# A hybrid recurrent and attention block on one core: the head's fillers, norm gain and first weights, and one copy at the entry of the up-projection

## The chip, the core and the metric

The kernel runs on one core of one Trainium2 chip. The metric is the device time of one execution in microseconds (us); of several runs the median is taken. Before the change it is 912.32 us (three runs, 912.11 to 912.33).

The engines are named as in the profile: PE is TensorE's matmul, PEld its weight load, DVE VectorE, ACT ScalarE, POOL GpSimd, SP SyncE. A "q" behind a name is the engine's sequencer, which waits and issues DMAs.

## What is computed

One layer over 512 tokens of 1024 channels, in float32:

```
h = rms_norm(x, mix_norm_pre)                 # x * rsqrt(mean(x^2) + eps) * gain
xa, ga, q, k, v, f, gA, gB = split(h @ w_in)
y_a = gelu(ga) * rg_lru(causal_conv4(xa));  y_b = forgetting_attention(q, k, v, f)
m = sigmoid(gA) * (y_a @ P_A) + sigmoid(gB) * (y_b @ P_B)
x = x + rms_norm(m @ w_out, mix_norm_post)
h = rms_norm(x, ffn_norm_pre)
up = causal_conv3(h @ w_up);  gate, val = split(up)
x = x + rms_norm((gelu(gate) * val) @ w_down, ffn_norm_post)
```

## The kernel before

**Arithmetic.** Every float32 product is made of three products in the reduced-precision type float32r. An operand `a` is split into a high part `ah` (a copy that rounds, `hi`, usually on ACT) and a low part `al = a - ah` (`lo`, on DVE or POOL), and `a*b` becomes `ah*bh + ah*bl + al*bh`. The class `Split` (L154) holds a block of weights: `raw` from DRAM by a DMA on SP (L166), `wh` from `hi` (L172), `wl` from `lo` (L175).

**Order of the work.** The stages stand one behind the other: the head (norm of x, its turning, and the first four blocks `xa0` to `xa3` of the input projection), then the rest of that projection with the recurrent gates, the attention, the merge, the output projection, the up-projection with conv and GLU, and the down-projection. Most of it is put in order by a scheduler that models times. The head (L576 to L685) and the up-projection from its entry on (L1373 to the end) stand under `manual_schedule`: each engine runs its instructions in the order in which the code gives them. An instruction that waits holds up all that stand behind it on its engine.

**The head** (L576 to L685). Token tiles `xt0` to `xt3` (128 tokens x 1024) and the first weights come in by SP's DMAs, the gain row `gone` (1 x 1024) by one of ACT's. What stands around the change:

- `spin(n)` (L594): n fillers on PE, products of nothing that is used, written into the bank that `xa3` takes later. Before, each is `ident x ident` in float32, 128 columns. `spin(6)` stands ahead of the gain products, `spin(1)` behind them.
- The gain row has to stand on all 128 partitions. DVE splits each half of `gone` into `gh` and `gl` of one row (L604, L605). PE multiplies a row of ones with them (L607), K = 1, so that a bank `pgain[i]` holds the half-row 128 times.
- Per token tile, `sumsq_whole` (L611) squares and sums on ACT and takes `rstd_of` (L237 and L239); `scaled` (L619) makes `x * rstd * gain` on DVE in two halves; `turn` (L246) transposes each half in four 128x128 pieces on PE into a bank; `evac_hi` (ACT, L250) copies it to `hh`, `evac_lo` (DVE, L254) the remainder to `hl`.
- `by_kind(0, X, ...)` (L638) multiplies block `xa0` with tokens 0 to 255 (`X`), kind after kind: `hh*wh`, then `hl*wh`, then `hh*wl`, eight products of 256 columns each. Its weights `wh_xa0` are rounded by ACT (`us[0].hi()`), `wl_xa0` is made by POOL (`us[0].lo(pool)`). Then `half(1, X)` does `xa1` (L230, L231, L233), and tiles 2 and 3 are turned.

**The entry of the up-projection** (L1373 to L1404). The up-projection uses a seven-product scheme on halves (class `Pair`, L341). `p.p5()` makes product 5 into the left half of bank `p.c`; `p.keep(1, ...)` (L436) copies that half to SBUF on ACT. In the first `period` (L454) PE goes on with `p.product(6, ...)` into the other bank, ACT keeps that one too (`keep(0)`), and `p.product(3, p.c[:, X])` then adds onto the half that `keep(1)` must have copied. `m.plain_low(0)` and `m.plain_high(0)` prepare weights of a later pair `m`: an ACT copy with a sign (L364), a DMA on POOL that adds onto it (L365), and an ACT copy that rounds (L380). `first_tap(0)` is two ACT instructions (L1325) on the first blocks.

Of the kernel before, what the change touches and what calls it, by code (L numbers as in the profile page):

```python
# [8 lines left out]
F32 = mybir.dt.float32  # L9
F32R = mybir.dt.float32r  # L10
BF16 = mybir.dt.bfloat16
AF = mybir.ActivationFunctionType
ALU = mybir.AluOpType
# [3 lines left out]
P = 128  # L17
S = 512
D = 1024
KD = D // P  # L20
# [43 lines left out]
def kernel(  # L64
# [16 lines left out]
    act, dve, pool, pe = nc.scalar, nc.vector, nc.gpsimd, nc.tensor  # L81
# [17 lines left out]
    def bank(name):  # L99
        return pspools[-1].tile([P, 512], F32, tag="ps", name=name)  # L100
# [4 lines left out]
    HALVES = (slice(0, 512), slice(512, 1024))  # L105

    ident = cpool.tile([P, P], F32, name="ident")
# [144 lines left out]
    def turned_lo(pv, t, g, ah, al):  # L252
        dst = (slice(None), slice(4 * g, 4 * g + 4), slice(t * P, (t + 1) * P))
        return dve.tensor_tensor(out=al[dst], in0=pv, in1=ah[dst].bitcast(F32), op=ALU.subtract)  # L254
# [67 lines left out]
    KH, SH = KD // 2, S // 2  # L322
# [5 lines left out]
    X, Y = slice(0, SH), slice(SH, S)  # L328
# [170 lines left out]
    with ExitStack() as rg:  # L499
        rt, ixt, tt = {}, {}, {}  # L500
        last_act = [None]
        with ExitStack() as r0:
            xpool = r0.enter_context(tc.tile_pool(name="xc", bufs=6, reuse_waits="tile"))
            gwpool = r0.enter_context(tc.tile_pool(name="rgw", bufs=2, reuse_waits="tile"))
            xc, xh, xl = {}, {}, {}
# [65 lines left out]
            with tc.tile_pool(name="pre", bufs=2, side="right", reuse_waits="tile") as pre, ExitStack() as wp:  # L571
# [6 lines left out]
                gone = pre.tile([1, D], F32, name="gone", bufs=1)  # L578
# [5 lines left out]
                us = [Split(*order[t][1:], order[t][0], wpre) for t in range(2)]  # L584
# [7 lines left out]
                pw = pss[3]  # L592

                def spin(n):  # L594
                    for i in range(n):
                        pe.matmul(pw[:, P * (i % 4) : P * (i % 4) + P], ident, ident, start=True, stop=True)

                spin(6)
                pgain = [bank(f"gain{i}") for i in range(2)]
                one = xpool.tile([P, S], F32R, tag="xc", name="one")[0:1, :P]  # L600
                pool.memset(one.bitcast(F32), 1.0)
                for i, c in enumerate(HALVES):
                    gh, gl = (xpool.tile([P, S], F32R, tag=x, name=f"gain_{x}{i}")[0:1] for x in ("xh", "xl"))
                    dve.tensor_copy(out=gh, in_=gone[:, c])  # L604
                    dve.tensor_tensor(out=gl, in0=gone[:, c], in1=gh.bitcast(F32), op=ALU.subtract)  # L605
                    for j, g in enumerate((gh, gl)):
                        pe.matmul(pgain[i], one, g, start=j == 0, stop=j == 1)  # L607

                xns, rss, ptr, lasts = {}, {}, {}, [None, None]

                def sumsq_whole(t):  # L611
                    xns[t] = pre.tile([P, D], F32, tag="xn", name=f"xn{t}")
                    ss = small.tile([P, 1], F32, tag="ss", name=f"ss_p{t}")
                    act.activation(out=xns[t], in_=xts[t], func=AF.Square, accum_out=ss)
                    rss[t] = rstd_of(ss, f"p{t}")
# [9 lines left out]
                def evac_hi(t, g):  # L625
                    lasts[0] = turned_hi(ptr[t, g], t, g, hh)

                def evac_lo(t, g):
                    lasts[1] = turned_lo(ptr[t, g], t, g, hh, hl)
# [4 lines left out]
                def by_kind(i, c, kinds):  # L634
                    wh, wl = us[i].parts()
                    for n, (w, h, k0, k1) in enumerate(kinds):
                        for k in range(k0, k1):
                            pe.matmul(pss[i][:, c], (wh, wl)[w][:, k], (hh, hl)[h][:, k, c],  # L638
                                      start=n == 0 and k == k0, stop=n == len(kinds) - 1 and k == k1 - 1)

                spin(1)
                sumsq_whole(0)
                scaled(0, 0)
                scaled(0, 1)
                turn(0, 0)
                turn(0, 1)
                sumsq_whole(1)
                us[0].hi()
                us[0].lo(pool)
                evac_hi(0, 0)  # L650
                evac_hi(0, 1)
                for g in range(2):
                    scaled(1, g)
                    turn(1, g)
                for g in range(2):
                    evac_lo(0, g)
                for g in range(2):
                    evac_hi(1, g)
                    evac_lo(1, g)
                by_kind(0, X, ((0, 0, 0, KD), (0, 1, 0, KD), (1, 0, 0, KD)))  # L660
                us[1].hi()
                us[1].lo(pool)
                sumsq_whole(2)
# [258 lines left out]
    with ExitStack() as g2:  # L922
# [17 lines left out]
        p, n = gp[0], gp[1]  # L940
# [39 lines left out]
    with ExitStack() as at:  # L980
# [141 lines left out]
        i = KD - 2  # L1122
# [38 lines left out]
    xpool = fstk.enter_context(tc.tile_pool(name="x2", bufs=1, reuse_waits="tile"))  # L1161
# [18 lines left out]
    with ExitStack() as mix:  # L1180
# [116 lines left out]
        with ExitStack() as later:  # L1297
            for i in turned[NT - 1]:
                later.enter_context(tc.issue_after(i.ins))
            p = pairs[NU]  # L1300
# [61 lines left out]
    def first_tap(j):  # L1362
        fe[j] = [tap(e, first[2 * j + i][0], t) for i, (e, t) in enumerate(((j, "cg"), (j + JF, "cv")))]

    def first_taps(j, *which):
        for i in which or (0, 1):
            taps(j + JF * i, first[2 * j + i][0], fe[j][i])
# [7 lines left out]
    p, n = pairs[NU], pairs[NU + 1]  # L1375
# [18 lines left out]
    p.add(p.a[:, X], p.a[:, X], 2)  # L1394
    first_tap(0)
    n.sums_lo(1)
    m.plain_low(0)
    m.plain_high(0)
    p.p5()
    p.keep(1, p.c[:, X])  # L1400
    first_taps(2)
    first_taps(0, 0)
    m.sums(0)
# [64 lines left out]
    with man2:  # L1468
# [3 lines left out]
        b, p = pairs.pop(JF - 2), pairs.pop(JF - 1)  # L1472
# [274 lines left out]
```

## Time and profile before

| what | value |
|---|---|
| median of the runs | 912.32 us |
| the profiled execution's own time | 910.93 us |
| its span, first to last instruction | 909.2 us |
| PE, PEld busy | 899.7 us (99%), 801.4 us (88%) |
| DVE, ACT, POOL busy | 736.5 (81%), 596.3 (66%), 214.8 us (24%) |
| chain that ended last | PE 98%, ACT 1%, DMA 1% |
| DMA | 185.24 MB, 204 GB/s over the span |

Times in the views are from the start of the span. In a row of a timeline stand the start, the length, the engine, the line, the operation, what it writes and reads, the shapes and how many were merged; behind it in brackets the idle time before it and what ended it. In a row of waits stand who waited for whom, the total, how often, and the longest. A matmul's length in such rows holds its way through the array, so that consecutive ones overlap: their rate is read from their starts.

### The profile page before, as it was taken

How to read it: one execution, taken by the hardware profiler on the slowest of the kernel's cores; microseconds unless marked ns; L12 is line 12 of the kernel's file. 1: busy time of each engine (PE TensorE's matmuls, PEld its weight loads, DVE VectorE, ACT ScalarE, POOL GpSimd, SP SyncE). 2: the span in 40 equal slices, each digit the busy share in tenths (PEclk: the TensorE clock that was granted, in tenths of full speed). 3: DMA queues.
4: the chain of work that ended last, by engine and by line, in shares of the span. 5: the costliest groups of instructions: out<-in, count | busy, mean ns of one | idle time of the engine just before them, and what ended most of it. 6: DMA issues, size and time to landing. Idle time of an engine off the chain costs nothing.

```text
span 909.2 us, 15828 instructions
## 1 busy us (share of the span) xinstructions
PE 899.7 (99%) x5858; PEld 801.4 (88%) x5858; DVE 736.5 (81%) x1204; ACT 596.3 (66%) x1032; POOL 214.8 (24%) x276
## 2 busy tenths in 40 slices
PE   9999999999999999999999999999999999999997
PEld 8888888878899998888888889999999999988886
DVE  6975469538878749888868588989999999889897
ACT  7564595333466648776654487878888888677564
POOL 3244335544110112212104100233323223100000
PEclk9999999999999999999999999999999999999999
DMA  6777589989865378444515664678888988699764
GB/s 261 263 237 195 159 221 272 247 215 197 196 161 161 101 245 280 143 143 149 177 45 183 200 185 139 140 185 209 235 210 215 244 203 210 209 400 324 244 203 145
DMA packets 71040, 185.24 MB, mean 204 GB/s; under 512 B 7153, under 2 KB 27681, under 8 KB 70578
## 3 DMA queue, kind: packets, MB, share of 16 engines
q1 hardware_dynamic: 47360, 127.72, 42.0%
q0 software_dynamic: 23456, 56.37, 28.7%
q8 instruction: 46, 0.75, 0.3%
q14 instruction: 32, 0.26, 0.1%
q10 hardware_dynamic: 146, 0.14, 0.0%
HBM read 150.69 MB, written 35.73 MB: 205 GB/s over the span
## 4 chain that ended last, share of the span: by engine, by line
PE 98%; ACT 1%; DMA 1%; DVE 0%; issue 0%; SPq 0%; DVEq 0%
PE up L429 7%; PE up L430 7%; PE up L432 7%; PE dn L1455 4%; PE dn L1456 4%; PE dn L1454 4%; PE ga L220 2%; PE ga L219 2%; PE pa L220 2%; PE pa L218 2%; PE pa L219 2%; PE ga L218 2%; PE k L218 2%; PE q L218 2%; PE wo L1170 2%; PE pb L218 2%
## 5 line engine op out<-in xcount | busy, mean ns | idle before, releaser
L1331 DVE SCALAR_TENSOR_TENSOR u<-up,cpt,u 128x511 f32<-128x511 f32 x96 | 71.3, 745 | 3.5 <-ACT u L1325 1.8
L365 POOL DMA_DIRECT2D ml<-raw_up x42 | 36.2, 863 | 153.6 <-ACT ml L364 87.2
L1456 PE MATMUL dn<-wh_dn,al 128*128 128x512 f32 (+1 forms) x180 | 67.6, 376 | 0.0
L1455 PE MATMUL dn<-wl_dn,ah 128*128 128x512 f32 (+1 forms) x180 | 67.5, 375 | 0.0
L1454 PE MATMUL dn<-wh_dn,ah 128*128 128x512 f32 (+1 forms) x180 | 67.5, 375 | 0.0
L429 PE MATMUL up<-sh,th 128*128 128x256 f32 x252 | 60.2, 276 | 0.0
L430 PE MATMUL up<-sl,th 128*128 128x256 f32 x252 | 60.2, 276 | 0.0
L175 DVE TENSOR_TENSOR wl_dn<-raw_dn,wh_dn 128x1024 fp32r<-128x1024 f32 x42 | 51.1, 1217 | 8.2 <-ACT wh_dn L172 8.2
L172 ACT CAST wh_dn<-raw_dn 128x1024 fp32r<-128x1024 f32 x42 | 44.1, 1051 | 20.2 <-issue 8.0
L1325 ACT ACTIVATE u<-up,cpt 128x512 f32<-128x512 f32 x48 | 37.0, 779 | 21.7 <-PE up L432 11.9
L325 DVE TENSOR_TENSOR tl<-t,th 128x1024 fp32r<-128x1024 f32 x42 | 51.1, 1217 | 0.0
L429 PEld LDWEIGHTS up<-sh,th 128*128 128x128 f32 x252 | 47.3, 188 | 0.0
L430 PEld LDWEIGHTS up<-sl,th 128*128 128x128 f32 x252 | 47.3, 188 | 0.0
L1339 POOL TENSOR_TENSOR yf<-u,u 128x512 f32<-128x512 f32 x23 | 30.7, 1334 | 62.8 <-issue 48.2
L411 ACT CAST th<-t 128x1024 fp32r<-128x1024 f32 x42 | 43.7, 1044 | 2.5 <-DVE t L325 0.4
L429 PE MATMUL up<-h2h,mh 128*128 128x256 f32 x168 | 40.2, 276 | 0.0
L430 PE MATMUL up<-h2l,mh 128*128 128x256 f32 x168 | 40.2, 276 | 0.0
L1456 PEld LDWEIGHTS dn<-wh_dn,al 128*128 128x128 f32 x180 | 33.9, 188 | 6.3 <-DVE al L325 0.3
L1454 PEld LDWEIGHTS dn<-wh_dn,ah 128*128 128x128 f32 x180 | 33.9, 188 | 6.1
L1455 PEld LDWEIGHTS dn<-wl_dn,ah 128*128 128x128 f32 x180 | 33.9, 188 | 6.0
L432 PE MATMUL up<-sh,tl 128*128 128x256 f32 x252 | 38.8, 276 | 0.0
L1015 ACT ACTIVATE P<-P,mx 128x384 f32<-128x384 f32 (+3 forms) x64 | 35.2, 553 | 5.1 <-DVE mx L1010 4.2
(724 smaller groups left out, 3218.9 us busy)
## 6 DMA issues: line engine op xcount, KB each, us to landing
raw_up<-in_w_up_dram SPq DMA_DIRECT2D x48, 512.0 KB, 5.4
td<-in_w_down_dram POOLq DMA_DIRECT2D x36, 512.0 KB, 6.3
raw_dn<-td SPq DMA_DIRECT2D x24, 512.0 KB, 5.3
ml<-raw_up POOLq DMA_DIRECT2D x21, 512.0 KB, 5.5
B<-cnd POOLq DMA_DIRECT2D x16, 640.0 KB, 5.4
raw_dn<-in_w_down_dram SPq DMA_DIRECT2D x18, 512.0 KB, 4.2
raw_wo<-in_w_out_dram SPq DMA_DIRECT2D x16, 512.0 KB, 4.3
td<-td POOLq DMA_DIRECT2D x12, 512.0 KB, 11.2
```

The costliest lines, as they stand in the source:

```text
L172: act.copy(self.wh, self.raw)
L175: engine.tensor_tensor(out=self.wl, in0=self.raw, in1=self.wh.bitcast(F32), op=ALU.subtract)
L218: pe.matmul(dst, ah, bh, start=first, stop=False)
L325: dve.tensor_tensor(out=out, in0=a, in1=b, op=ALU.subtract)
L411: act.copy(self.th[i], self.t[i])
L429: pe.matmul(dst, wh[:, k], ah[:, k], start=first and k == 0, stop=False, skip_group_check=True)
L430: pe.matmul(dst, wh[:, k], al[:, k], start=False, stop=False, skip_group_check=True)
L432: pe.matmul(dst, wl[:, k], ah[:, k], start=False, stop=k == KH - 1, skip_group_check=True)
L1331: dve.scalar_tensor_tensor(out=c[:, s:], in0=ps[:, : S - s], scalar=col(C_CFW + 3 * e + j), in1=c[:, s:], op0=ALU.mult, op1=ALU.add)
L1454: pe.matmul(d[:, x], ah[:, k, tok], wh[:, k, x], start=first, stop=False, skip_group_check=True)
L1455: pe.matmul(d[:, x], ah[:, k, tok], wl[:, k, x], start=False, stop=False, skip_group_check=True)
L1456: pe.matmul(d[:, x], al[:, k, tok], wh[:, k, x], start=False, stop=last, skip_group_check=True)
```

## The change

In the head:

- A tile `ones` of 128x512 is set by DVE. A filler is now a 128-row product of it with itself, 512 columns. Five stand ahead of the gain products and seven behind them, in place of six and one. POOL's `memset` of a row of ones goes.
- The gain parts `gh` and `gl` are now four tiles of 128 rows, set to zero by DVE ahead of the split; the split writes row 0. The product with `ones` then has K = 128.
- `wh_xa0` is rounded by POOL instead of ACT, and `wl_xa0` follows on POOL in two halves of 512 columns (L652 to L655 of the changed file).
- `by_kind(0, X, ...)` takes `hl*wh` and `hh*wl` in halves over k, alternating; DVE's `evac_lo` follows that order.

At the entry of the up-projection, `p.p5()` and `p.keep(1, ...)` stand ahead of `m.plain_low(0)` and `m.plain_high(0)`.

```diff
--- before.py
+++ after.py
@@ -593,18 +593,22 @@
 
                 def spin(n):
                     for i in range(n):
-                        pe.matmul(pw[:, P * (i % 4) : P * (i % 4) + P], ident, ident, start=True, stop=True)
-
-                spin(6)
+                        pe.matmul(pw, ones[:, :P], ones, start=True, stop=True)
+
+                ones = xpool.tile([P, S], F32R, tag="xc", name="ones")
+                dve.memset(ones.bitcast(F32), 1.0)
+                spin(5)
                 pgain = [bank(f"gain{i}") for i in range(2)]
-                one = xpool.tile([P, S], F32R, tag="xc", name="one")[0:1, :P]
-                pool.memset(one.bitcast(F32), 1.0)
+                gtiles = [[xpool.tile([P, S], F32R, tag=x, name=f"gain_{x}{i}") for x in ("xh", "xl")] for i in range(2)]
+                for pair in gtiles:
+                    for g in pair:
+                        dve.memset(g.bitcast(F32), 0.0)
                 for i, c in enumerate(HALVES):
-                    gh, gl = (xpool.tile([P, S], F32R, tag=x, name=f"gain_{x}{i}")[0:1] for x in ("xh", "xl"))
-                    dve.tensor_copy(out=gh, in_=gone[:, c])
-                    dve.tensor_tensor(out=gl, in0=gone[:, c], in1=gh.bitcast(F32), op=ALU.subtract)
+                    gh, gl = gtiles[i]
+                    dve.tensor_copy(out=gh[0:1], in_=gone[:, c])
+                    dve.tensor_tensor(out=gl[0:1], in0=gone[:, c], in1=gh[0:1].bitcast(F32), op=ALU.subtract)
                     for j, g in enumerate((gh, gl)):
-                        pe.matmul(pgain[i], one, g, start=j == 0, stop=j == 1)
+                        pe.matmul(pgain[i], ones[:, :P], g, start=j == 0, stop=j == 1)
 
                 xns, rss, ptr, lasts = {}, {}, {}, [None, None]
 
@@ -638,26 +642,27 @@
                             pe.matmul(pss[i][:, c], (wh, wl)[w][:, k], (hh, hl)[h][:, k, c],
                                       start=n == 0 and k == k0, stop=n == len(kinds) - 1 and k == k1 - 1)
 
-                spin(1)
+                spin(7)
                 sumsq_whole(0)
                 scaled(0, 0)
                 scaled(0, 1)
                 turn(0, 0)
                 turn(0, 1)
                 sumsq_whole(1)
-                us[0].hi()
-                us[0].lo(pool)
+                pool.tensor_copy(out=us[0].wh, in_=us[0].raw)
+                for c in HALVES:
+                    pool.tensor_tensor(out=us[0].wl[:, c], in0=us[0].raw[:, c], in1=us[0].wh[:, c].bitcast(F32),
+                                       op=ALU.subtract)
                 evac_hi(0, 0)
                 evac_hi(0, 1)
                 for g in range(2):
                     scaled(1, g)
                     turn(1, g)
                 for g in range(2):
-                    evac_lo(0, g)
-                for g in range(2):
                     evac_hi(1, g)
-                    evac_lo(1, g)
-                by_kind(0, X, ((0, 0, 0, KD), (0, 1, 0, KD), (1, 0, 0, KD)))
+                    for t in range(2):
+                        evac_lo(t, g)
+                by_kind(0, X, ((0, 0, 0, KD), (0, 1, 0, KH), (1, 0, 0, KH), (0, 1, KH, KD), (1, 0, KH, KD)))
                 us[1].hi()
                 us[1].lo(pool)
                 sumsq_whole(2)
@@ -1394,10 +1399,10 @@
     p.add(p.a[:, X], p.a[:, X], 2)
     first_tap(0)
     n.sums_lo(1)
+    p.p5()
+    p.keep(1, p.c[:, X])
     m.plain_low(0)
     m.plain_high(0)
-    p.p5()
-    p.keep(1, p.c[:, X])
     first_taps(2)
     first_taps(0, 0)
     m.sums(0)
```

How this moves rows. PE, from the program's first instruction to the end of `by_kind(0, X)`; `xa` with the fillers is the bank of `xa3`, `tr_p` the banks of the turned tiles. Before:

```order
L596 MATMUL xa_172<-ident 128x128 x6
L607 MATMUL gain_179<-gain_xh_183,one 128x512
L607 MATMUL gain_179<-gain_xl_184,one 128x512
L607 MATMUL gain_180<-gain_xh_189,one 128x512
L607 MATMUL gain_180<-gain_xl_190,one 128x512
L596 MATMUL xa_172<-ident 128x128
L246 MATMUL tr_p_0_205<-ident,xn_196 128x128 x4
L246 MATMUL tr_p_1_210<-ident,xn_196 128x128 x4
L246 MATMUL tr_p_0_227<-ident,xn_215 128x128 x4
L246 MATMUL tr_p_1_233<-ident,xn_215 128x128 x4
L638 MATMUL xa_169<-hh,wh_xa_151 128x256 x8
L638 MATMUL xa_169<-hl,wh_xa_151 128x256 x8
```

The same stretch of PE's queue in the changed kernel:

```order
L596 MATMUL xa_172<-ones 128x512 x5
L611 MATMUL gain_180<-gain_xh_182,ones 128x512
L611 MATMUL gain_180<-gain_xl_183,ones 128x512
L611 MATMUL gain_181<-gain_xh_184,ones 128x512
L611 MATMUL gain_181<-gain_xl_185,ones 128x512
L596 MATMUL xa_172<-ones 128x512 x7
L246 MATMUL tr_p_0_214<-ident,xn_205 128x128 x4
L246 MATMUL tr_p_1_219<-ident,xn_205 128x128 x4
L246 MATMUL tr_p_0_237<-ident,xn_224 128x128 x4
L246 MATMUL tr_p_1_243<-ident,xn_224 128x128 x4
L642 MATMUL xa_169<-hh,wh_xa_151 128x256 x8
L642 MATMUL xa_169<-hl,wh_xa_151 128x256 x4
```

Seven fillers of 512 columns stand between the gain products and the first transpose, where one of 128 columns stood; `hl*wh` comes in two groups of four, and `hh*wl`, four at a time, behind each of them.

ACT, at the entry of the up-projection; `u` with `up` and `cpt` is `first_tap(0)`, `x_3` what `keep` writes for pair 3, `ml_5` and `mh_5` the weights of `m`. Before:

```order
L436 COPY x_3_6816<-up_6791 128x256
L1325 ACTIVATE u_6819<-up_6243,cpt 128x512
L1325 ACTIVATE u_6821<-up_6268,cpt 128x512
L364 ACTIVATE ml_5_6825<-raw_up_6777 128x1024
L380 CAST mh_5_6828<-raw_up_6777 128x1024
L436 COPY x_3_6843<-up_6830 128x256
L436 COPY x_3_6866<-up_6791 128x256
```

ACT there in the changed kernel:

```order
L436 COPY x_3_6826<-up_6801 128x256
L1330 ACTIVATE u_6829<-up_6253,cpt 128x512
L1330 ACTIVATE u_6831<-up_6278,cpt 128x512
L436 COPY x_3_6848<-up_6835 128x256
L364 ACTIVATE ml_5_6850<-raw_up_6787 128x1024
L380 CAST mh_5_6853<-raw_up_6787 128x1024
L436 COPY x_3_6876<-up_6801 128x256
```

The copy of product 5's half (`up_6830`, now `up_6835`) has gone ahead of the two weight instructions. PE's, DVE's and POOL's orders at this place are the same as before.

## The prediction

> **What bounds the kernel now.** First the page: its span, its busy times, the chain that ended last. Then the waits of PE over the whole span.
>
> ```profile
> span 909.2 us, 15828 instructions
> PE   899.7 (99%) x5858; PEld 801.4 (88%) x5858; DVE 736.5 (81%) x1204; ACT 596.3 (66%) x1032; POOL 214.8 (24%) x276
> PE 98%; ACT 1%; DMA 1%; DVE 0%; issue 0%; SPq 0%; DVEq 0%
> ```
> ```profile
> PE xa L596 <- POOL ident masks.py:199: 1.5, 1, 1.5
> PE up L429 <- ACT x L436: 1.2, 1, 1.2
> ```
>
> PE is the bound from end to end, and it waits twice: 1.5 us for the first filler's operand, and 1.2 us once, for the copy `keep`. So the change can gain that one wait, and what PE does too slowly in the head; everything behind a gain moves forward with PE, unless a wait appears there. The durations are from the profiled execution, whose own time is 910.93 us (909.2 us of span and 1.7 around it); the median of the runs is 912.32, 1.4 above. I take the difference worked out here off the median.
>
> **The entry of the up-projection.** The timeline at PE's wait:
>
> ```profile
> 588.31 1.46 ACT L1325 ACTIVATE u<-up,cpt 128x512 f32<-128x512 f32 x2
> 588.75 0.62 PE L432 MATMUL up<-sh,tl 128*128 128x256 f32 x4
> 589.65 1.06 ACT L364 ACTIVATE ml<-raw_up 128x1024 fp32r<-128x1024 f32 x1
> 590.11 0.62 PE L432 MATMUL up<-sh,tl 128*128 128x256 f32 x4
> 590.60 1.04 ACT L380 CAST mh<-raw_up 128x1024 fp32r<-128x1024 f32 x1
> 591.53 0.66 ACT L436 COPY x<-up 128x256 f32<-128x256 f32 x2
> 591.97 0.38 PE L429 MATMUL up<-sh,mh 128*128 128x256 f32 x1 [1.24 <-ACT x L436]
> ```
>
> The first PE row is the end of product 5: over at 588.75 + 0.62 = 589.37. The second ends product 6; its four starts lie 0.113 apart (the same rows of two products lie 1.36 us apart, for 12 matmuls), so product 3 could begin at 590.11 + 4 x 0.113 = 590.56. It begins at 591.97, because its bank half is copied by the first of the two ACT copies, which stand behind `ml` and `mh`. That costs **1.41 us**.
>
> After the change the copy starts when ACT leaves the taps, at 589.65, when product 5 has been over for 0.28 us, and takes some 0.38: done at 590.03, half a microsecond before PE wants it. So the whole 1.41 goes. Behind it on ACT stand `ml` and `mh`, each some 0.27 us later (the distance at which the two copies follow each other), with POOL's DMA for `ml`; the other copy keeps its time, since ACT has the same work ahead of it. That copy releases product 7, which comes after product 3 and two more products (some 4.1 us after 590.56), 2.5 us after the copy ends at 592.2. Nothing is late next by these rows; later waits are for ACT and DVE work that PE itself sets off, and moves with it. Bounds: 0 (a wait of the same size stands up behind) to 1.41; I take 1.41.
>
> **The head.** The stretches of the head by engine, then its rows:
>
> ```profile
> 1.49:6.99 5.50, 5.50 (x18) 4.29 (x18) 3.13 (x7) 3.87 (x8) 0.00 (x0) 1.00 0.91 323
> ```
> ```profile
> 0.74 0.20 POOL masks.py:197 MEMSET ident<- 128x128 f32 x1 [0.29 <-POOLq L1734]
> ...
> 1.49 2.93 PE L596 MATMUL xa<-ident 128*128 128x128 f32 x12 [1.49 <-POOL ident masks.py:199]
> 2.31 0.41 DVE L604 CAST gain_xh<-gone 1x512 fp32r<-1x512 f32 x1 [2.31 <-DMA gone<-in_gains_dram]
> 3.81 0.68 DVE L605 TENSOR_TENSOR gain_xl<-gone,gain_xh 1x512 fp32r<-1x512 f32 x1
> 5.38 0.62 PE L607 MATMUL gain<-gain_xh,one 1*128 1x512 f32 x1
> 5.80 0.62 PE L607 MATMUL gain<-gain_xl,one 1*128 1x512 f32 x1
> 6.13 1.41 DVE L619 SCALAR_TENSOR_TENSOR xn<-xt,rs_p,gain 128x512 f32<-128x512 f32 x2
> 7.03 3.36 PE L246 MATMUL tr_p<-ident,xn 128*128 128x128 f32 x16
> 7.65 1.41 DVE L619 SCALAR_TENSOR_TENSOR xn<-xt,rs_p,gain 128x512 f32<-128x512 f32 x2
> 7.92 1.04 ACT L172 CAST wh_xa<-raw_xa 128x1024 fp32r<-128x1024 f32 x1 [0.72 <-DMA raw_xa<-in_w_in_dram]
> 8.87 2.13 ACT L250 CAST hh<-tr_p 128x512 fp32r<-128x512 f32 x4
> 9.05 2.40 POOL L175 TENSOR_TENSOR wl_xa<-raw_xa,wh_xa 128x1024 fp32r<-128x1024 f32 x1 [7.61 <-ACT wh_xa L172]
> 9.49 2.48 DVE L254 TENSOR_TENSOR hl<-tr_p,hh 128x512 fp32r<-128x512 f32 x4 [0.43 <-ACT hh L250]
> 10.49 1.29 PE L638 MATMUL xa<-hh,wh_xa 128*128 128x256 f32 x8
> 13.43 0.19 PEld L230 LDWEIGHTS xa<-hh,wh_xa 128*128 128x128 f32 x1
> 16.37 1.91 PE L246 MATMUL tr_p<-ident,xn 128*128 128x128 f32 x16
> ```
>
> Sixteen transposes take 3.36 us at 7.03 and 1.91 at 16.37; a 512-column product follows the last after 0.42 (5.38 to 5.80), twice the 0.23 that 256 columns in 0.113 would make. So PE runs at half speed until about 10 us, though it is busy all through from 1.49 to 6.99. The granted clock's column (the last but two) reads 1.00 there and doesn't show it; the rows' rate does. `xa0`'s products begin at 10.49, behind transposes and ACT's four copies, and `xa1` follows at 13.43. That last number is what the head gives on.
>
> [...]
>
> Added durations, bounded by the nearest rows:
>
> ```profile
> L1025 DVE TENSOR_SCALAR P<-P,sm 128x512 f32<-128x512 f32 x16 | 7.9, 495 | 0.5
> L821 POOL MEMSET f_ones<- 16x512 f32 x1 | 0.5, 517 | 0.0
> masks.py:197 POOL MEMSET ident<- 128x128 f32 x1 | 0.2, 205 | 0.3 <-POOLq L1734 0.3
> masks.py:199 POOL TENSOR_SCALAR_AFFINE_SELECT ident<-ident 128x128 f32<-128x128 f32 x1 | 0.3, 284 | 0.0
> ```
>
> *DVE's memset of 128x512*: 0.41 (the one-row cast) to 0.70 (half of the row of two at 6.13); I take 0.5, by `TENSOR_SCALAR`. *POOL's cast of 128x1024*: 1.03 (twice the 512-column memset) to 2.40 (two inputs); with one input, 284 to 205 at 128 columns, 1.03 x 1.39 = 1.4; taken. [...] *A half of `wl`*: 1.33, by a row of the page with its operation and shape:
>
> ```profile
> L1339 POOL TENSOR_TENSOR yf<-u,u 128x512 f32<-128x512 f32 x23 | 30.7, 1334 | 62.8 <-issue 48.2
> ```
>
> **Step by step.** DVE is free from about 0.75, as POOL is (its 0.74 row); five memsets end at 3.25, so the splits start 0.94 later than 2.31 and the last ends at 3.81 + 0.68 + 0.94 = 5.43. PE starts its fillers at 1.3 instead of 1.49; five of 0.43 end at 3.45, then PE waits for the splits (about 1 us in all), and the last gain product starts at 5.47, before 5.80: DVE's `scaled` keeps its place. Seven fillers follow at 5.90. At half speed they end at 8.91; at full speed from 6.5 (1.4 of them by then, 5.6 x 0.23 after), at 7.8. I choose 6.5: full-row work from 1.3 on, less its hole, has then run as long as the full-row work from about 6.4 to 9.9 that came ahead of full speed before. Transposes: 7.8 to 9.71 at the 16.37 row's rate, instead of 7.03 to 10.39. ACT, free of the 1.04 cast, starts its copies at 7.8 + 0.48 + 0.15 (8.4), and the third is done at 10.05, the fourth at 10.55. `hh*wh`: two fours from 10.05 and 10.55, ending at 11.0. POOL: cast 7.92 to 9.3, halves to 10.7 and 12.0. Then four `hl*wh` to 11.5, four `hh*wl` to 11.95, four `hl*wh` to 12.45 (DVE's fourth remainder, four of 0.62 behind ACT's third copy, at 12.0), four `hh*wl` to 12.9. `xa1` starts at 12.9 instead of 13.43: **0.5 us**. POOL's `wl_xa1` (2.4 from 12.0: 14.4) is in time: it is wanted 16 x 0.113 after 12.9, at 14.7. If it were not, PE would wait there for POOL. On SP the two loads of gate weights go behind one more weight load, and their first reader, on ACT, comes ten microseconds later:
>
> ```profile
> 11.84 0.91 SPq L529 DMA_DIRECT2D graw<-in_rgw_dram  x2
> ...
> 25.60 1.13 ACT L530 CAST gh<-graw 128x512 fp32r<-128x512 f32 x2
> ```
>
> The old fillers and POOL's memset of a row lay ahead of 5.80 and of the first transpose; their going is in the steps above, and so are PE's seven fillers, which no other work hides: they cost whatever part of them lies past 6.9, where `scaled` delivers the first transpose's operand.
>
> Bounds of the head: +0.8 (memset 0.41, full speed by 6.5 and transposes at 7.4); below nothing, the rivals.
>
> **Sum.** 1.41 + 0.5 = 1.9: 912.32 - 1.9 = **910.4**.
>
> **The rivals.**
>
> *The cold stretch is longer in the timed runs.* They are 1.4 above the profiled execution. If full speed came a step later there, half-rate products until past 13 would explain it, and the full-row fillers save up to 1.3 more: 909.1. For: the gap. Against: a fixed overhead would do.
>
> *Full speed comes no earlier* (by the count of busy time, the fillers change nothing). Fillers to 8.9, five transposes by 9.95, the other eleven to 11.3; ACT's fourth copy is done at 12.0 (0.15 and 0.58 later), and the twenty products behind it end at 14.3: the head loses 0.9, and 0.5 is left: 911.8. [...]
>
> *POOL's cast takes 2.4.* `wh` at 10.3, halves at 11.7 and 13.0, `xa1` at 13.5: the head loses 0.1: 911.0.
>
> *The entry's wait comes back behind.* 0.5 left: 911.8. Against it stand the margins above.
>
> [...]
>
> **How the numbers follow.** Forecast 0.54 (909.9 to 910.9), longer cold stretch 0.15, no earlier 0.11, long cast 0.09, wait comes back 0.05, slower 0.06. The range, 909.0 to 911.9, holds all but the slow case and about half of the three at its ends. A measurement of this kernel can tell 0.2% (1.8 us) from no change; so faster means below 910.5: the longer cold stretch and two thirds of the forecast, 0.51. Slower, above 914.1, is past the slow case's price: its far end, 0.02. The rest, 0.47, is within.
>
> **What would show it.** PE's wait for `x L436` gone, the copy ahead of `ml` and done near 590 less the head's gain; the transposes' sixteen in about 1.9 us; the seven fillers over before 8; POOL's cast row below 1.8; `xa1`'s first weight load at 12.9. Wrong if transposes still take 3.4, if PE stands between fillers and transposes, or if a new wait of PE appears after the entry.

## The result, and the profile after

The changed kernel takes **909.61 us** in the median of nine runs (909.04 to 910.34). Nine runs of the kernel before beside it take 912.11 (911.3 to 913.43). The ratio is 0.9976, 95% interval 0.9967 to 0.9984: 2.2 us faster. The prediction was 910.4, between 909.0 and 911.9. In a later comparison on one chip (e10 below) the same kernel comes out at 0.9982 (0.9973 to 0.9991), 1.6 us faster; before stood there at 911.55, and in the two other comparisons at 911.62. Half a microsecond of the first difference is thus before's own median in that comparison.

The profiled execution of the changed kernel takes 909.84 us, with a span of 908.0. From its page, the span, the busy times and the chain that ended last:

```profile
span 908.0 us, 15830 instructions
PE 899.4 (99%) x5856; PEld 800.0 (88%) x5856; DVE 739.0 (81%) x1209; ACT 594.9 (66%) x1031; POOL 215.9 (24%) x277
PE 99%; DVE 0%; ACT 0%; issue 0%; DVEq 0%
```

What PE waited for, over the whole span:

```profile
PE xa L596 <- DVE ones L599: 1.5, 1, 1.5
PE xa L642 <- ACT hh L250: 0.4, 1, 0.4
PE k L218 <- DVE mx L1015: 0.2, 1, 0.2
```

The wait for `x L436` is gone. In its place stands nothing at the entry, but two new rows stand in the list: 0.4 us in the head, ahead of `xa0`, and 0.2 in the attention.

**The entry.** The timeline of the changed kernel there:

```profile
588.72 1.46 ACT L1330 ACTIVATE u<-up,cpt 128x512 f32<-128x512 f32 x2
589.16 0.62 PE L432 MATMUL up<-sh,tl 128*128 128x256 f32 x4
590.06 0.38 ACT L436 COPY x<-up 128x256 f32<-128x256 f32 x1
590.31 1.09 ACT L364 ACTIVATE ml<-raw_up 128x1024 fp32r<-128x1024 f32 x1
590.52 0.62 PE L432 MATMUL up<-sh,tl 128*128 128x256 f32 x4
590.98 0.28 PE L429 MATMUL up<-sh,mh 128*128 128x256 f32 x1
592.21 0.40 ACT L436 COPY x<-up 128x256 f32<-128x256 f32 x1
```

PE arrives here 0.41 later than in the profile of before (product 5 begins at 588.25, and in before at 587.84). With that taken off, the copy runs from 589.65 to 590.03, to the hundredth where the prediction put it; it ends 0.54 before product 3, which follows product 6 without a gap. The other copy, at 592.21, keeps its place. The stretch from product 5's first product to the down-projection's first product, in before and then in the changed kernel; the columns are the stretch, its length, and busy time (and count) of PE, PEld, DVE, ACT, POOL, then PE's granted clock and the DMA share and rate:

```profile
587.84:786.02 198.18, 196.94 (x1730) 196.74 (x1729) 181.27 (x265) 159.05 (x244) 59.19 (x60) 1.00 0.84 215
```
```profile
588.25:784.93 196.68, 196.68 (x1730) 196.68 (x1729) 181.06 (x265) 158.70 (x244) 59.20 (x60) 1.00 0.84 215
```

198.18 becomes 196.68: 1.50 us, of which 1.24 was PE's idle time, and 0.26 busy time. Of the latter, 0.16 is the tail of product 6's last row: the row is 0.276 long, and the next product starts 0.113 after it when nothing holds it. The other 0.10 is a slow start behind the wait: there the first product has a row of 0.38, and the second starts 0.22 after it (591.97, 592.19); without the wait it starts 0.12 after it (590.98, 591.10).

**The head.** The changed kernel's timeline:

```profile
0.92 0.48 DVE L599 MEMSET ones<- 128x512 f32 x1 [0.92 <-PEq L1739]
1.46 2.50 PE L596 MATMUL xa<-ones 128*128 128x512 f32 x5 [1.46 <-DVE ones L599]
3.08 0.48 DVE L605 MEMSET gain_xl<- 128x512 f32 x1
3.48 0.35 DVE L608 CAST gain_xh<-gone 1x512 fp32r<-1x512 f32 x1
5.66 0.80 PE L611 MATMUL gain<-gain_xl,ones 128*128 128x512 f32 x1
6.25 2.19 PE L596 MATMUL xa<-ones 128*128 128x512 f32 x7
6.30 1.41 DVE L623 SCALAR_TENSOR_TENSOR xn<-xt,rs_p,gain 128x512 f32<-128x512 f32 x2
7.04 1.04 POOL L652 CAST wh_xa<-raw_xa 128x1024 fp32r<-128x1024 f32 x1 [5.73 <-DMA raw_xa<-in_w_in_dram]
8.17 2.54 POOL L654 TENSOR_TENSOR wl_xa<-raw_xa,wh_xa 128x512 fp32r<-128x512 f32 x2
8.28 1.91 PE L246 MATMUL tr_p<-ident,xn 128*128 128x128 f32 x16
8.92 2.05 ACT L250 CAST hh<-tr_p 128x512 fp32r<-128x512 f32 x4 [1.54 <-PE tr_p L246]
10.62 1.18 PE L642 MATMUL xa<-hh,wh_xa 128*128 128x256 f32 x8 [0.43 <-ACT hh L250]
13.41 0.19 PEld L230 LDWEIGHTS xa<-hh,wh_xa 128*128 128x128 f32 x1
```

The transposes are fast (1.91 for sixteen, before 3.36), POOL's cast is short, and yet `xa1`'s first weight load stands at 13.41, before at 13.43. The row to read is the seven fillers: they hold PE until 8.28, although the transposes' first operand is there at 6.30 + 0.70 = 7.0. So ACT's first copy starts at 8.92. Before, it started at 8.87, behind the cast that ACT is now free of. In this pair of profiles, what the clock and the freed ACT gave, the fillers took.

### The profile page after: what moved, and what is told of

Its sections match the earlier page's. It is cut to its first block, busy times and chain, and to the rows that moved or that the text cites. A ratio compares the mean times of both kernels' runs of the same rounds, so it can differ in the third digit from the quotient of the medians.

```text
span 908.0 us, 15830 instructions
## 1 busy us (share of the span) xinstructions
PE 899.4 (99%) x5856; PEld 800.0 (88%) x5856; DVE 739.0 (81%) x1209; ACT 594.9 (66%) x1031; POOL 215.9 (24%) x277
## 4 chain that ended last, share of the span: by engine, by line
PE 99%; DVE 0%; ACT 0%; issue 0%; DVEq 0%
PE up L430 7%; PE up L432 7%; PE up L429 7%; PE dn L1461 4%; PE dn L1460 4%; PE dn L1459 4%; PE pa L218 2%; PE ga L220 2%; PE ga L218 2%; PE pa L219 2%; PE pa L220 2%; PE ga L219 2%; PE k L218 2%; PE q L218 2%; PE wo L1175 2%; PE pb L218 2%
```

## The experiments

Three sets (e1 to e4, e5 to e8, e9 to e11), each on one chip and beside runs of before (33, 27 and 21 of them, medians 911.62, 911.62 and 911.55). All results in one table: the time, the ratio to before, and from each profile the start of full clock (from the trace's record of the granted clock), the starts of the first and the last of the first sixteen transposes, of the first product of `xa0` and of `xa1`.

| kernel | us, median (range; runs) | ratio, 95% | full clock | transposes | `xa0` | `xa1` |
|---|---|---|---|---|---|---|
| before | above | | 9.95 | 7.03 to 10.11 | 10.49 | 13.54 |
| after, first profile | 909.61 (909.04–910.34; 9) | 0.9976 [0.9967, 0.9984] | 7.12 | 8.28 to 9.92 | 10.62 | 13.53 |
| e1 entry alone | 909.79 (909.55–911.31; 11) | 0.9983 [0.9974, 0.9992] | 10.81 | 6.99 to 10.21 | 10.46 | 13.77 |
| e2 head alone | 911.36 (910.86–912.93; 11) | 0.9999 [0.9990, 1.0008] | 7.23 | 8.34 to 9.98 | 10.69 | 13.56 |
| e3 weights alone | 911.52 (910.71–912.93; 11) | 1.0001 [0.9992, 1.0010] | 12.32 | 7.25 to 10.48 | 10.81 | 14.40 |
| e4 fillers alone | 911.91 (911.01–912.88; 11) | 1.0001 [0.9992, 1.0010] | 5.04 | 7.62 to 9.64 | 10.00 | 13.18 |
| e5 after, two fillers | 909.64 (909.30–910.35; 8) | 0.9976 [0.9966, 0.9986] | 5.98 | 7.13 to 9.60 | 10.04 | 13.01 |
| e6 after, POOL zeros, four | 909.63 (909.23–910.61; 7) | 0.9972 [0.9961, 0.9983] | 9.41 | 8.09 to 10.38 | 11.03 | 13.94 |
| e7 after, fifteen fillers | 911.65 (910.97–913.34; 12) | 1.0000 [0.9991, 1.0008] | 5.22 | 9.43 to 11.07 | 11.77 | 14.65 |
| e8 two fillers, weights on ACT | 910.56 (910.12–912.94; 12) | 0.9987 [0.9979, 0.9995] | 6.56 | 7.17 to 9.64 | 10.43 | 13.49 |
| e9 after, eight products less | 907.98 (907.60–909.88; 5) | 0.9964 [0.9952, 0.9977] | 6.34 | 7.91 to 9.68 | 10.26 | 13.16 |
| e10 after again | 909.95 (909.01–910.67; 11) | 0.9982 [0.9973, 0.9991] | 7.61 | 8.49 to 10.12 | 10.83 | 13.73 |
| e11 entry alone again | 909.81 (909.03–910.68; 11) | 0.9984 [0.9975, 0.9992] | 10.39 | 7.24 to 10.44 | 10.71 | 13.85 |

An interval is about 0.9 us to either side, so what is below that is read from the profiles, not from the times.

### The parts by themselves (e1 to e4)

The first comparison showed 2.5 us between the medians, and the entry's wait was only 1.4 of it. e1 is before with the entry's edit, e2 the changed kernel with the old entry:

```diff
-    m.plain_low(0)
-    m.plain_high(0)
     p.p5()
     p.keep(1, p.c[:, X])
+    m.plain_low(0)
+    m.plain_high(0)
```

e3 is before with only the weights' part of the head (POOL's cast, the halves of `wl_xa0`, the alternating order of `by_kind` and `evac_lo`); e4 is before with only the other part (the tile `ones`, the gain tiles of 128 rows, five and seven fillers).

> The kernel before with the copy moved up alone, the head as it was. Theory A (the entry's wait is worth its 1.4 us, the rest of the change's 2.5 comes from an earlier full clock in the head): 1.4 us faster than the kernel before. Rival B (the rest comes from ACT being freed of the first rounding): 1.4 faster as well. Rival C (the entry is worth all of it, since the profiled head ends at the same 13.4 us in both kernels): 2.5 faster.

> The head of the changed kernel with the entry of before. Theory A: 1.1 us faster than the kernel before, as a median over runs whose clock rises at different times, though a profile in which the clock of before rose early shows nothing. Rival B: 1.1 faster. Rival C: within 0.3.

> Of the change only the first weights on GpSimd in halves, with the order of the kinds and remainders that goes with it; fillers, gain and entry as before. Theory A: within 0.3 us of before, since at half clock the transposes end at 10.4 and not ACT but they hold the first product. Rival B: 1.1 faster. Rival C: within 0.3.

> Of the change only the ones tile, the zeroed gain tiles and the five and seven long fillers; first weights on ACT and the entry as before. Theory A: about 1.1 us faster in the median, full clock at about 7 us in the profile instead of about 10. Rival B: 0 or slower, since seven fillers hold the first transpose to 8.3. Rival C: within 0.3.

e1 is 1.5 us faster, e2, e3 and e4 are level with before. So theories A and B, which both gave the head 1.1 us, fall; C is nearest, with the entry as all of it, though not with the 2.5 it gave the entry. The stretch from product 5 to the down-projection has the same length in e1's profile as in the changed kernel's, and in e2's the same as in before's:

```profile
588.11:784.79 196.68, 196.68 (x1730) 196.68 (x1729) 181.06 (x265) 158.95 (x244) 59.13 (x60) 1.00 0.85 216
```
```profile
588.94:787.13 198.19, 196.95 (x1731) 196.75 (x1729) 181.29 (x265) 158.88 (x244) 59.15 (x60) 1.00 0.85 215
```

e3 shows why a free ACT alone is worth nothing. Its head, with the old fillers:

```profile
7.25 3.65 PE L246 MATMUL tr_p<-ident,xn 128*128 128x128 f32 x16
8.38 0.59 ACT L250 CAST hh<-tr_p 128x512 fp32r<-128x512 f32 x1 [0.96 <-PE tr_p L246]
9.23 0.59 ACT L250 CAST hh<-tr_p 128x512 fp32r<-128x512 f32 x1 [0.27 <-PE tr_p L246]
10.08 0.59 ACT L250 CAST hh<-tr_p 128x512 fp32r<-128x512 f32 x1 [0.27 <-PE tr_p L246]
```

ACT starts its first copy half a microsecond earlier than before, and then waits ahead of every copy for transposes at half speed (3.65 us for sixteen; 1.91 at full clock). (Full clock came later here than in any other profile, at 12.32, so that what this part is worth in other executions is read from its time, 1.0001.) In e4 the clock is up at 5.04, and the fillers run at full speed; the transposes end half a microsecond earlier than before, and `xa1` starts 0.36 earlier, which its time, at 1.0001, doesn't show:

```profile
6.00 1.79 PE L596 MATMUL xa<-ones 128*128 128x512 f32 x7
7.62 2.29 PE L246 MATMUL tr_p<-ident,xn 128*128 128x128 f32 x16
8.26 2.28 ACT L250 CAST hh<-tr_p 128x512 fp32r<-128x512 f32 x4
```

### The number of fillers (e5 to e8)

If the seven fillers take what the head was to gain, fewer must bring it out, and more must cost. The edit to the changed kernel in e5:

```diff
-                spin(7)
+                spin(2)
```

e7 has `spin(15)` there, and e6 `spin(4)` together with

```diff
-                        dve.memset(g.bitcast(F32), 0.0)
+                        pool.memset(g.bitcast(F32), 0.0)
```

e8 has two fillers, and the weights' part taken back (ACT rounds `wh_xa0`, POOL makes `wl_xa0` in one piece, the old order of kinds).

> The changed kernel with two fillers behind the gain products instead of seven. Theory F (the seven fillers eat what the head was to gain: in the changed kernel's trace the first transpose's operand is there at 7.0 us and the fillers end at 8.28): transposes start at 7.1, ACT's third copy ends at 9.7, xa1's first product stands at 12.75 instead of 13.53, and the time is 0.8 us below the changed kernel's. Rival G (the head does not set the pace, a later wait gives it back): xa1 earlier, but the time as the changed kernel's within 0.3. Rival J (the fillers are needed to keep the clock up): the clock rises at 10 or later, the transposes take over 3 us, xa1 at 13.7 and the time 0.2 above the changed kernel's.

> The changed kernel with the four gain tiles zeroed by POOL instead of DVE (DVE's splits then begin at 2.3 instead of 3.48, as before the change) and four fillers behind the gain products instead of seven. Theory F: the gain products end near 5, the four fillers by 6.7, transposes start at 7.05, xa1 at 12.7, the time 0.8 us below the changed kernel's (and 2.3 below that of before). Rival G: the time as the changed kernel's within 0.3. Rival J: as the changed kernel's or above, with the clock's rise at 10 or later.

> The changed kernel with fifteen fillers behind the gain products instead of seven, a dose. Theory F: eight more at 0.23 us each, full clock: transposes at 10.1, xa1 at 15.3, the time 1.8 us above the changed kernel's. Rival G: the head's delay is taken up later, the time less than 0.9 above the changed kernel's. Rival J: 1.8 above less what an earlier clock saves, so as F within 0.3.

> The changed kernel with two fillers instead of seven, and the first weights rounded on ACT and their low part made on POOL in one piece again, in the order of before: the fillers without the weights' part. Theory F: ACT's copies start behind the cast at 8.4 instead of 7.7, the third still ends near 9.8; the low parts come in the old order, so that xa1 starts at 13.1: 0.4 below the changed kernel, 0.4 above the kernel with two fillers and POOL's cast. Rival G: the changed kernel's time within 0.3. Rival J: 0.2 to 0.6 above the changed kernel's.

**The dose costs** (e7). Eight more fillers bring the time from 0.9976 or 0.9982 back to 1.0000, by 1.6 to 2.2 us, where 1.8 was expected; G, which let the rest absorb it, falls. In its profile `xa1` is only 1.1 later than in the changed kernel's, because the clock rose at 5.22 there, before the fillers began. Their row:

```profile
5.99 3.60 PE L596 MATMUL xa<-ones 128*128 128x512 f32 x15
9.43 1.91 PE L246 MATMUL tr_p<-ident,xn 128*128 128x128 f32 x16
```

**Fewer bring the head forward, but the time stays** (e5). The head with two:

```profile
6.13 0.63 PE L596 MATMUL xa<-ones 128*128 128x512 f32 x2
7.13 1.22 PE L246 MATMUL tr_p<-ident,xn 128*128 128x128 f32 x8 [0.38 <-DVE xn L623]
7.80 1.18 ACT L250 CAST hh<-tr_p 128x512 fp32r<-128x512 f32 x2 [0.48 <-PE tr_p L246]
8.65 1.22 PE L246 MATMUL tr_p<-ident,xn 128*128 128x128 f32 x8 [0.29 <-DVE xn L623]
9.31 1.18 ACT L250 CAST hh<-tr_p 128x512 fp32r<-128x512 f32 x2 [0.33 <-PE tr_p L246]
10.04 1.25 PE L642 MATMUL xa<-hh,wh_xa 128*128 128x256 f32 x8 [0.17 <-ACT hh L250]
```

Transposes and copies start as F said, at 7.13 and 7.80; the second tile's wait for DVE's `xn` makes them start again at 8.65, so that `xa1` stands at 13.01 instead of the 12.75 expected, 0.52 ahead of the changed kernel's. J falls: the clock was up at 5.98. But the time is the changed kernel's. The profiles show where the lead goes, the gate products near 328 us. Product by product e5 stands 0.5 ahead of the changed kernel from 15 us on; at 328.8 it is 0.02 behind, and 0.29 from 333 on:

```profile
326.12 1.05 ACT L172 CAST wh_q<-raw_q 128x1024 fp32r<-128x1024 f32 x1 [1.30 <-DMA raw_q<-in_w_in_dram]
327.20 1.23 DVE L175 TENSOR_TENSOR wl_q<-raw_q,wh_q 128x1024 fp32r<-128x1024 f32 x1 [1.92 <-ACT wh_q L172]
328.35 0.89 DVE L448 TENSOR_TENSOR mb<-mb,gx 128x256 f32<-128x256 f32 x2
328.82 0.39 PE L429 MATMUL mb<-hh,gth 128*128 128x256 f32 x1 [0.32 <-DVE mb L448]
```

The load of `raw_q` lands no earlier than in the changed kernel, where ACT takes it at 325.87, held by PE and not by the load; its cast holds up DVE's split, this the addition onto `mb`, and this PE.

**e6** gave nothing that can be told either. Its splits began no earlier than with the memsets on DVE, as the gain row came late in this execution:

```profile
3.41 0.42 DVE L608 CAST gain_xh<-gone 1x512 fp32r<-1x512 f32 x1 [2.01 <-DMA gone<-in_gains_dram]
```

Its clock rose at 9.41, so that even four fillers held PE until 8.09. That profile comes near what J expected (a rise at 10 or later), and at 910.61 it is the slowest of its seven runs; the other six take 909.23 to 909.79.

**e8** keeps ACT's cast ahead of the copies, and `xa1` comes 0.48 after e5's (13.49, expected 0.35 after): with few fillers the move of the cast to POOL is worth that in the head. By the times e8 is 1.0 us slower than e5, but its profile doesn't tie this to the head: at the down-projection's first product it is level with e5 (785.13, then 785.20), and the 0.7 by which its span is longer is lost at 797 to 802 us, in the down-projection. What holds PE there is not shown.

### Does a shorter head get through? (e9 to e11)

e9 makes PE early by a known amount: in block `xa2` the products of `hh` with the low weights are left out. e10 and e11 are the changed kernel and the entry alone once more, on the same chip.

```diff
-                for t in (2, 3):
-                    project(pss[t], us[t].parts(), hh, hl)
+                wh, wl = us[2].parts()
+                for k in range(KD):
+                    pe.matmul(pss[2], wh[:, k], hh[:, k], start=k == 0, stop=False)
+                    pe.matmul(pss[2], wh[:, k], hl[:, k], start=False, stop=k == KD - 1)
+                project(pss[3], us[3].parts(), hh, hl)
```

> The changed kernel with the products of the high part of h with the low weights left out in block xa2: eight products of 512 columns, 0.227 us each, so that PE is 1.82 us ahead from about 31 us on. It stands for a head that is 1.8 us shorter. Theory F (a head that ends earlier would move all of the rest): the first attention score at 336.7 instead of 338.5 and the time 1.8 us below the changed kernel's. Rival G (the loads and the gate products near 260 and 329 us don't move along, as in the trace with two fillers, where 0.5 us of head was given back at 328.8 by a wait for the load of raw_q): the score at 338.0 or later and the time at most 0.9 below the changed kernel's.

> The changed kernel itself, on the chip and in the rounds of the entry alone. Theory C' (the head gives nothing): within 0.4 us of the entry alone. Theory A' (the head gives the 0.5 of the prediction, but the run of the head alone was too unsure to show it): 0.5 below the entry alone. Theory D (the fillers cost): 0.3 or more above the entry alone.

> The entry alone again, in the same rounds as the changed kernel: 1.4 to 1.6 us below before by its ratio if the wait for the copy of product 5's half is all that it removes. Theories of the head as with the changed kernel in the same rounds.

e9 is 1.97 us below e10 by the medians, and 1.6 by the ratios, where F said 1.8 and G at most 0.9. Its first attention score stands at 337.06, in the two profiles of the changed kernel at 338.51 and 339.14. From `xa3`'s first product to the last product of the kernel, in e9's profile and then in e10's:

```profile
27.02:899.33 872.31, 871.88 (x5688) 776.33 (x5687) 712.52 (x1162) 574.31 (x995) 202.50 (x262) 1.00 0.72 203
```
```profile
29.57:901.73 872.16, 871.91 (x5688) 776.18 (x5687) 711.22 (x1158) 574.24 (x995) 203.62 (x262) 1.00 0.72 202
```

The lead of 2.55 us (1.82 left out, the rest a quicker head in that execution) is 2.40 at the end: 0.15 is given back. At the gate products where e5 waited, e9 waits too, 0.43 us; most of that comes back behind, where e10 has a wait of 0.2 for `mx` and e9 none. So G falls for a lead of this size: most of it reaches the end, less some tenths. Of a lead that is itself some tenths, as e5's, this says little. The changed kernel and the entry alone are level: 909.95 and 909.81, ratios 0.9982 and 0.9984. C' holds: the head as it is gives nothing; A' and D, at 0.5 below and 0.3 above, are not borne out, though the intervals don't exclude them.

One place takes from the changed head what it gains. Product by product, the changed kernel's first profile stands 0.32 to 0.36 ahead of e11's from 15 us to 340, 0.15 from the `k` products near 341 on, and is level from 348.6 on. The two places together take 0.35 to 0.38 in seven profiles (both of the changed kernel, e2, e4, e5, e7, e8), against e11's, and nothing in before, e1, e3, e6 and e9. So e10 has this loss and e9 does not; by these figures e9 would have kept 2.04 of its lead of 2.55 with it, which is an estimate. The rows of DVE's first pass over the scores and of PE's product that then waits, in the changed kernel and in e11:

```profile
339.96 0.69 DVE L1015 CUSTOM_DVE_ANT_0 P<-s0c,B 128x512 f32<-128x512 f32 x1 [2.52 <-PE s1c L1006]
340.81 0.47 PE L218 MATMUL k<-hh,wh_k 128*128 128x512 f32 x1 [0.17 <-DVE mx L1015]
```
```profile
339.97 0.69 DVE L1010 CUSTOM_DVE_ANT_0 P<-s0c,B 128x512 f32<-128x512 f32 x1 [2.07 <-PE s1c L1001]
340.93 0.50 PE L218 MATMUL k<-hh,wh_k 128*128 128x512 f32 x1
```

DVE starts 1.45 us behind the first score (338.51) in the changed kernel, and 1.11 behind it (338.86) in e11. It is 1.45 to 1.48 in the seven profiles, and 1.10 to 1.11 in the six others: the four with the old fillers, e6 and e9. The named releaser, `s1c`, is through at 339.47 in the changed kernel, so that something else held DVE there, and why this comes with the new fillers, but not in e6 and e9, is not shown.

## Why the prediction came out right, and its step that was wrong

**The entry** was right in mechanism and size: 1.41 worked out, 1.50 in the profiles (the stretch from product 5 to the down-projection takes 198.18 to 198.21 in the four with the old entry, 196.67 to 196.69 in the nine with the new one), 1.5 by the ratios of e1 and of e11. The missing 0.09 is the slow start of the first product behind the wait (0.10), which the sum from start to start at that place leaves out. Nothing was late next; the rival of the wait that comes back behind falls.

**The head** was mis-sized: 0.5 predicted, 0.02 in the profiled pair, 0.2 over the profiles of the two heads (`xa1` at 13.72 in the mean of before, e1 and e11, at 13.50 in that of the changed kernel, e2, e9 and e10), and in the times nothing that can be told (0.1 faster by e2's ratio, 0.1 slower by the medians of e10 against e11). The step that failed is "Seven fillers follow at 5.90 ... at full speed from 6.5 (...), at 7.8". They began at 6.25: DVE's first memset starts at 0.92 and the five follow each other every 0.54 (taken: 0.75 and 0.5), so that the last gain product came at 5.66, not 5.47, and the first filler followed it after 0.59, not 0.43. Full clock came at 7.12; the 6.5 was an estimate, and the five profiles with these twelve fillers have 5.04 to 7.61. The fillers held PE until 8.28, 0.5 later than worked out (by the rates taken there, an estimate, 0.2 of it for the late start and 0.3 for the late clock), and everything behind them came as much later: ACT's first copy 8.92 for 8.4, `xa0` 10.62 for 10.05, `xa1`'s weight load 13.41 for 12.9. The order of the terms was right; the 0.5 of gain was just the 0.5 of this delay. The fillers' cost, "whatever part of them lies past 6.9", was 0.9 in the sum and is 1.3 in this profile; e7 shows it from the other side. A second step failed behind the head: "everything behind a gain moves forward with PE, unless a wait appears there". A wait appeared, the 0.17 for `mx` at 340.81, and with it 0.36 us were lost near 341 and 348.6, in the first profile just what the changed kernel was ahead of e11.

**The rest of the difference** between 910.4 and 909.61 is not the head. Of the 2.5 us between the first medians 1.5 is the entry; 0.5 is the median of before in that comparison against the three later ones; the rest is within the interval. So it is in part luck that the measured time lies below the forecast and not above it: the head's 0.5 did not come, and a median of before that stood half a microsecond high made up for it.

**The rivals.** *Full speed no earlier* falls: sixteen transposes take 1.91 in the changed kernel, and the last of e10's starts at 10.12 after a first at 8.49. *POOL's cast takes 2.4* falls: 1.04, at the low end of the bounds (twice the 512-column memset), and not the 1.4 taken by the affine select's ratio. *Slower* (0.06 of the chances) falls: full clock came at 7.12, DVE's memset took 0.48, PE's holes among the gain products stayed below 0.3 (the longest step between their starts is 0.71, where products without a hole stand 0.43 apart). *A longer cold stretch in the timed runs* did not show: with it e2 would have gained up to 1.3, and it is at 0.9999. One step later than 9.95 is 13.36 by the steps of 3.413 in the clock's record (below), and the latest start in a profile is e3's 12.32. The cold stretch does differ between executions with the same fillers (9.95, 10.81, 12.32 and 10.39 with the old ones). Where it was longest, in e3, `xa1` came 0.86 later than in before's profile, and that execution, at 912.93, is the slowest of e3's runs; how much of this is the clock's was not tested.

**What is open.** In the twelve profiles other than e9's the stretch from `xa2`'s first product to the first attention score takes between 314.6 and 315.7 us; single waits of 0.2 to 0.5 us near 260 and 329 come and go, also between the two profiles of the changed kernel. A head 0.5 us shorter, as in e5, is of that size. The loss near 341 and 348.6 stands in both profiles of the changed kernel, and its cause is open. Whether the two-filler version is faster than the changed kernel is not settled by these runs (0.9976 both), and none of the kernels tried that compute all of the products is shown to beat it.

## What to carry to other kernels

Look for an engine's one wait in the list of waits, and see in the timeline what stands ahead of the released instruction in its queue: where a copy stands behind work that nobody needs yet, moving it up can be worth the whole wait. Here it was worth the 1.41 us and 0.1 more, as the second product behind the wait started 0.22 after the first, and 0.12 without the wait. Fillers that are there for the clock alone are on the path as soon as their end passes the arrival of what the engine really waits for (here 8.28 against 7.0): count them from the late side of the clock's start (5.04 to 9.41 in the nine profiles with full-row fillers). Before trusting a gain of half a microsecond at the front, see how far the middle of the kernel varies by itself, and whether it gives the gain back at one place in every profile of the new kernel.

## What the runs showed of the hardware

**When full clock comes.** In the four profiles with the old fillers it came at 9.95 to 12.32, in eight of the nine with full-row fillers at 5.04 to 7.61 (e6: 9.41). The old work ahead of the transposes (1-row products, float32 products of 128 columns) kept PE busy from 1.49 on (5.50 of the 5.50 us to 6.99 in before's profile), and full clock was not there at its end; it came 2.9 to 5.1 us after the first transpose. From its start to its fall after the last product the record has 897.705 us in before and in the changed kernel's first profile, 894.292 in e1 and e3, 901.119 in e4, e7 and e8: 263, 262 and 264 steps of 3.413 us. The place of the start differs between executions of one kernel (7.12 and 7.61 in the changed kernel, 10.81 and 10.39 in the entry alone). In before's profile one step ahead of 9.95 is 6.54, an estimate from these lengths: full clock did not come there, though PE had been busy throughout the 3.41 us before it, 2.0 of them with 1-row products. What makes it come is not shown.

**GpSimd's cast** of 128x1024 from float32 to float32r took 1.04 us in the changed kernel's profile, where the prediction took 1.4.

**DVE's memset** of 128x512 float32 took 0.48 in its row and 0.54 from one to the next.
